# Moving activations and split weights 64 bytes apart in a 128-byte grid

## The chip, the core and the metric

The kernel runs on one NeuronCore of a Trainium2 chip. The metric is the device time of one execution in microseconds (us). A core has five engines that run side by side: TensorE (PE in the profile, with its weight loads listed as PEld), VectorE (DVE), ScalarE (ACT), GpSimd (POOL) and SyncE (SP, which here issues the DMAs). On-chip memory (SBUF) has 128 partitions. A tile takes the same range of byte addresses in every partition, so "the address of a tile" below is one number, its first byte within a partition.

## The reference, cut to what matters

Two layers of a transformer-like block over 256 tokens of width 1024, in float32. Each layer has a token mixer with three branches and an MLP:

```python
h = rms_norm(x, g_pre_mix) * (1.0 + sc_m) + sh_m
proj = h @ w_in                       # 1024 x 11272: rq rk rv rg lx ly fq fk fv ff gates
...                                   # retention, RG-LRU and forgetting attention
merged = g[:, :, 0] * (y_ret @ ret_w_o) + g[:, :, 1] * (y_lru @ lru_w_o) + g[:, :, 2] * (y_fox @ fox_w_o)
x = x + gt_m * rms_norm(merged @ w_out, g_post_mix)
h = rms_norm(x, g_pre_mlp) * (1.0 + sc_f) + sh_f
f = jnp.square(jax.nn.relu(h @ w1)) @ w2          # 1024 x 4096, 4096 x 1024
return x + gt_f * rms_norm(f, g_post_mlp)
```

Nearly all the work is matrix products of the 256 x 1024 activations with weights that are read once from memory. The shift, scale and gate columns come from further products with `ada_w`.

## The kernel before, in words

**Split operands.** Every float32 operand of a product is split into two float32r tiles, a high part and the remainder, and a product is three matmuls (`mm3`): high by high, high by low, low by high.

```python
def mm3(ps, ah, al, bh, bl, start, stop, **kw):
    T.matmul(ps, ah, bh, start=start, stop=False, **kw)      # L341
    T.matmul(ps, ah, bl, start=False, stop=False, **kw)      # L342
    T.matmul(ps, al, bh, start=False, stop=stop, **kw)       # L343
```

The first of the two operands is the stationary one: TensorE loads its 128 x 128 block with a weight load (LDWEIGHTS) ahead of each matmul. The second is the moving one, whose columns stream through.

**Two shapes of product.** `gemm` keeps a weight block stationary and streams 256 tokens of an activation (`hh`/`hl`, `yrh`/`yrl` and so on; the tiles in the profile's names stand in the order moving, stationary: `ps<-hh,whi`). `gemm_wide` and `gemm_n` keep 128 tokens of the activation stationary and stream the weights, 512 columns a matmul (256 in `gemm_n`; 264 in the one product of `fv` with the eight columns of `ff` beside it, whose output tiles are called `pf`). The MLP's `w2`, the first quarter of `w1`, `rv` and `w_o` take the wide form, the rest the other.

**Weights.** SyncE's queue brings each half of a weight block into one of five `wraw` tiles; `split` makes the high part on ACT (L217) and the remainder on DVE (L218). The pair goes to `whi`/`wlo` of the weight pool `wp`, or, where the table `SLOTS` or the list `SPARE_SLOTS` names a slot, into a `wown` tile in one of the activation slots.

**Activation slots.** The pool `up` has twelve slots of 8192 bytes per partition, `T1` to `T10`, `hh` and `hl`. `U(tag, shape, dt, name)` makes a tile in a slot. All activations that TensorE reads, except the small probability tiles `pth`/`ptl` and the gates' `uh`/`ul`, live there.

**Addresses.** The pools are laid out one after the other: `cpool` (constants, `sir`, the residual `xs`), `wp`, `up`, `tp` (scratch), `sp` (small columns). All tiles of `wp` and `up` begin at multiples of 128 bytes, and the rows within them are 512, 1024, 2048 or 4096 bytes long. One tile is an exception: `fv`'s first weight block is `[128, 4, 264]`, so its row `k` (one block of 128 input channels) begins 1056 `k` bytes, that is 32 `k` bytes past a multiple of 128. `sir` and `xs` begin 64 bytes past a multiple, since `csb` (8704 bytes) and `vsb` (1216 bytes) stand ahead of them. The constants' `csb` and `pth`/`ptl` begin at multiples.

**What sets the order.** The program is written out in one order (`mix_order`, `mlp_order`), weights are loaded two or three blocks ahead, and the work on heads is woven in between products by `side`. Each engine then runs its own list in order and waits on semaphores of the others.

Of the kernel before, what the change touches and what calls it, by code (L numbers as in the profile page):

```python
# [10 lines left out]
F32 = mybir.dt.float32  # L11
F32R = mybir.dt.float32r
# [2 lines left out]
ALU = mybir.AluOpType  # L15
PSUM = bass.MemoryType.PSUM
KH = 4
NRAW = 5
NHL = 4
PL = None  # L20
# [11 lines left out]
P = 128  # L32
D = 1024
KD = D // P
S = 256
L = 2
FF = 4 * D
NH_R = 4
NH_F = 8
C = 256  # L40
# [27 lines left out]
def mix_order(l):  # L68
    first = 'g0 g0 g0 g0 lx lx g1 lx g1 lx lru' if l == 0 else \
            'rv rv rv rv rq rk g0 rq rk g0 lx g0 lx g0 lx g1 lx lru g1'  # L70
    rest = 'rg rg rg rg g1 w_r w_r w_r w_r g1 ly ly ly ly fq w_l w_l w_l w_l fv fv fv fv fq fq fq fk fk fk fk ' \
           'g2 g2 g2 g2 w_f w_f w_f w_f w_o w_o w_o w_o'
    order = first.split() + rest.split()
    return [(n, order[:i].count(n)) for i, n in enumerate(order)]
# [8 lines left out]
def wide(name, cix):  # L83

    return name in ('rv', 'w_o', 'w2') or (name == 'w1' and cix < 4)
# [31 lines left out]
def trunk_kernel(ctx, tc, x, c, vec, con, ffw, wts, out):  # L117
# [4 lines left out]
    up = ctx.enter_context(tc.tile_pool(name="up", bufs=1))  # L122
# [5 lines left out]
    pz = ctx.enter_context(tc.tile_pool(name="pz", bufs=2, space=PSUM))  # L128

    V, A, T = nc.vector, nc.scalar, nc.tensor  # L130

    csb = cpool.tile([P, NCON], F32, name="csb")
    vsb = cpool.tile([P, L, NVEC], F32, name="vsb")
# [29 lines left out]
    both = cpool.tile([P, NH_F], F32, name="both")  # L163
# [35 lines left out]
    def raw_half(i, extra=None):  # L199
        n = C if extra is None else C + NH_F  # L200
        t = wp.tile([P, KH, n], F32, name="wraw", tag="wraw", bufs=NRAW)
        src = wts[pos[0], i]
        if extra is None:
            nc.sync.dma_start(t.rearrange("p k c -> p (k c)"), src)
        else:
            nc.sync.dma_start(t[:, :, :C], src.rearrange("p (k c) -> p k c", k=KH))
            nc.sync.dma_start(t[:, :, C:], extra[:, i * KH:(i + 1) * KH, :])
        return t
# [3 lines left out]
    def split_tiles(n):  # L212
        return (wp.tile([P, KH, n], F32R, name="whi", tag="whi", bufs=NHL),
                wp.tile([P, KH, n], F32R, name="wlo", tag="wlo", bufs=NHL))

    def split(t, hi, lo):
        A.copy(hi, t)  # L217
        V.tensor_tensor(lo, t, hi.bitcast(F32), ALU.subtract)  # L218
# [11 lines left out]
    def split_of(l, name, cix):  # L230
        parts = []
        for i in range(2):
            t = early.pop(0) if early else raw_half(i, ffw[l] if (name, cix) == ('fv', 0) else None)
            n = t.shape[-1]
            if (name, cix) in SLOTS:
                own = SLOTS[name, cix][i]
            elif name in ('w1', 'w2') and (name, cix) < ('w2', 12):
                own = SPARE_SLOTS[spare[0] % len(SPARE_SLOTS)]
                spare[0] += 1
            else:  # L240
                own = PL
            if own:
                both = U(own, [P, 2, KH, C], F32R, "wown")
                hi, lo = both[:, 0], both[:, 1]
            else:
                hi, lo = split_tiles(n)
            split(t, hi, lo)
            parts.append((hi, lo))
        pos[0] += 1
        if wide(name, cix):  # L250
            parts = [[p.rearrange("p (k j) c -> p k (j c)", k=2) for p in hl] for hl in parts]
            return [(parts[k // 2][0][:, k % 2, :], parts[k // 2][1][:, k % 2, :]) for k in range(KH)]
        return [(parts[k // KH][0][:, k % KH, :], parts[k // KH][1][:, k % KH, :]) for k in range(KD)]
# [143 lines left out]
            lates = [evac(banks[t][j], t, j) for j in range(2)]  # L397
        return lates

    def U(tag, shape, dt, name):  # L400
        return up.tile(shape, dt, name=name, tag=tag)

    def tmp(tag, name, dt=F32, shape=(P, 2, S), **kw):
        return tp.tile(list(shape), dt, name=name, tag=tag, **kw)
# [225 lines left out]
    def mixer(l, nm, h=None, rvp=None, qkp=None):  # L630
        hh, hl = h or nm.h

        def G(name, i, x=None, natural=False):
            prefetch(3 if name in DEEP else 2)
            side(BUDGET[name])
            w = weight(l, name, i)
            ps = pa.tile([P, 2, S], F32, name="ps", tag="a") if name in LONG else None
            return (gemm_n if natural else gemm)(w, *(x or (hh, hl)), ps)

        def pair(i):  # L640
            return slice(2 * i, 2 * i + 2)
# [55 lines left out]
        qk = {}  # L697
# [102 lines left out]

            first_quad(l, 'rv', nm, rv_quad)

        qk.update(rq=U("T1", [P, 2, NH_R, S], F32R, "rq"), rk=U("T2", [P, 2, NH_R, S], F32R, "rk"))
        heads = []

        def rope(name, i, ps):
            t = qk[name]
            sw = tmp("t1", "sw")
            A.copy(sw[0:64], ps[64:128])
            A.copy(sw[64:128], ps[0:64])  # L810
            r = tmp("t2", "ro")
            V.tensor_tensor(r, ps, cn('cos')[:, None, :].to_broadcast([P, 2, S]), ALU.mult)
            V.tensor_tensor(sw, sw, cn('sin')[:, None, :].to_broadcast([P, 2, S]), ALU.mult)
            yield 1.2
            V.tensor_tensor(r, r, sw, ALU.add)
            A.copy(t[:, 0, pair(i), :], r)
            lo(t[:, 1, pair(i), :], r, t[:, 0, pair(i), :])
            yield 1.2

        def add_heads(i, *after):  # L820
            heads.extend(Side(ret_head(h), *after, *heads[h - NPT:h - NPT + 1]) for h in (2 * i, 2 * i + 1))
            if i == 1:
                heads.append(Side(ret_norm(), *heads))
# [3 lines left out]
        def gate_evac(b, i):  # L827
            if i == 0:
                gate[b] = U("T9" if b else "T10", [P, KD, S], F32, "gate")
            A.activation(gate[b][:, pair(i), :], G(f'g{b}', i), AF.Tanh, scale=0.5)  # L830
# [133 lines left out]
        for n, i in mix_order(l):  # L964
            if n in ('rq', 'rk'):
                for _ in rope(n, i, G(n, i)):
                    pass
                if n == 'rk':
                    add_heads(i)
            elif n in ('g0', 'g1', 'g2'):  # L970
                gate_evac(int(n[1]), i)
            elif n == 'lx':
                if (l, i) == (0, 0):
                    lru_consts()
                conv(i)
            elif n == 'lru':
                for h in heads[:NH_R]:
                    finish(h)
                wl.append(weight(l, 'lru', 0))
                gs = [Side(lru_gates(j)) for j in range(4)]  # L980
            elif n == 'rg':
                if i == 0:
                    finish(heads[-1])
                    yr = U("T1", [P, KD, S], F32R, "yrh"), U("T2", [P, KD, S], F32R, "yrl")
                ret_gate(i, yr)
            elif n == 'w_r':
                if i == 0:
                    rec = Side(recurrence(), *gs)
                merge(0, 'w_r', i, yr)
            elif n == 'ly':  # L990
                if i == 0:
                    finish(rec)
                    yl = U("T3", [P, KD, S], F32R, "ylh"), U("T4", [P, KD, S], F32R, "yll")
                gelu_gate(i, yl)
            elif n == 'w_l':
                merge(1, 'w_l', i, yl)
            elif n == 'fq':
                if (l, i) == (0, 0):
                    V.tensor_tensor(both, ident[:, 0:NH_F], ident[:, CUM_LO:CUM_LO + NH_F], ALU.add)
                    A.mul(sel, both, -1.0)  # L1000
                if i == 0:
                    fq = U("T1", [P, NH_F, S], F32R, "fqh"), U("T2", [P, NH_F, S], F32R, "fql")
                fox_q(i, *fq)
            elif n == 'fv':
                if i == 0:
                    fv = U("T3", [P, 2, D], F32R, "fvh"), U("T4", [P, 2, D], F32R, "fvl")
                fox_v(i, *fv)
            elif n == 'fk':
                if i == 0:
                    fk = U("T5", [P, NH_F, S], F32R, "fkh"), U("T6", [P, NH_F, S], F32R, "fkl")  # L1010
                    yf = U("T7", [P, KD, S], F32R, "yfh"), U("T8", [P, KD, S], F32R, "yfl")
                fox_k(i, *fk)
            elif n == 'w_f':
                if i == 0:
                    side()
                    mh, ml = U("T1", [P, KD, S], F32R, "mh"), U("T2", [P, KD, S], F32R, "ml")
                    nm = Norms(l, 'm', (l, 'f'), ("T3", "T4", "T7"))
                merge(2, 'w_f', i, yf)
                ks = pair(i)
                A.mul(mh[:, ks, :], gate[0][:, ks, :], 0.5)  # L1020
                V.scalar_tensor_tensor(ml[:, ks, :], gate[0][:, ks, :], 0.5, mh[:, ks, :].bitcast(F32), ALU.mult,
                                       ALU.subtract)
# [163 lines left out]
```

## Time and profile before

| | |
|---|---|
| three runs | 1155.24, 1156.79, 2241.36 us; median 1156.79 |
| the profiled execution | 1157.0 us, its span 1155.2 us |
| TensorE busy | 1130.4 us, 98% of the span, 8164 matmuls |
| weight loads | 1066.6 us, 92% |
| DVE, ACT, POOL busy | 873.4 (76%), 617.9 (53%), 33.8 us (3%) |
| DMA | 255.43 MB, mean 221 GB/s |
| mean granted TensorE clock | 0.999 |

The span is what the profiler sees between the first and the last instruction; the execution's time holds 1.8 us more around it. Matmuls overlap in the profile: one is listed with the time from its issue to its end (some 283 ns for 256 columns), while the next one starts much earlier. How fast TensorE goes is therefore read from the distance between starts.

### The profile page before, as it was taken

The numbers are of one execution on the slowest core, as the hardware profiler recorded it, in microseconds if no ns is written. First come the engines' busy times: TensorE is split into PE (matmuls) and PEld (weight loads), VectorE is DVE, ScalarE is ACT, GpSimd is POOL, SyncE is SP. The second block draws the span as 40 slices with busy tenths as digits, with TensorE's granted clock in tenths as the row PEclk, the third lists the DMA queues.
The fourth block names the chain that finished last, engine by engine and source line by source line (L and its number), as shares of the span: only waits on it lengthen the run. The fifth ranks groups of instructions, "written<-read, shape, count | busy, mean of one in ns | idle before, by whom it ended". The sixth has DMA issues, their size and how long they took to land.

```text
span 1155.2 us, 20486 instructions
## 1 busy us (share of the span) xinstructions
PE 1130.4 (98%) x8164; PEld 1066.6 (92%) x8164; DVE 873.4 (76%) x1323; ACT 617.9 (53%) x912; POOL 33.8 (3%) x54
## 2 busy tenths in 40 slices
PE   6999999999999999999999999999999999999997
PEld 5999999999999889989879999999999997989986
DVE  6898788878787789887586768877777778866543
ACT  6676594544465555444555658655444645645432
POOL 0001000000000100000010010000000002000000
PEclk9999999999999999999999999999999999999999
DMA  9954546579876569998645454566777574875641
GB/s 364 390 181 148 183 135 210 180 245 315 282 242 221 194 221 320 335 308 297 236 157 172 151 194 148 167 199 185 232 264 253 180 276 146 274 244 187 192 150 67
DMA packets 74284, 255.43 MB, mean 221 GB/s; under 512 B 10108, under 2 KB 12492, under 8 KB 74188
## 3 DMA queue, kind: packets, MB, share of 16 engines
q1 hardware_dynamic: 74188, 254.12, 65.1%
q8 instruction: 64, 1.05, 0.4%
q14 instruction: 32, 0.26, 0.1%
HBM read 253.00 MB, written 1.09 MB: 220 GB/s over the span
## 4 chain that ended last, share of the span: by engine, by line
PE 82%; DMA 7%; DVE 4%; issue 4%; POOL 1%; ACT 1%; DVEq 0%; POOLq 0%; SPq 0%; ACTq 0%
PE ps L341 24%; PE ps L343 24%; PE ps L342 24%; DMA wraw<-in_wts_dram 7%; DVE wlo L218 2%; DVE wraw L273 1%; PE xT L421 1%; PE rvp L341 1%; PE rvp L342 1%; PE qkp L343 1%; PE qkp L341 1%; PE qkp L342 1%; PE rvp L343 1%; POOL rs_v L186 1%; POOL rs_r L187 0%
## 5 line engine op out<-in xcount | busy, mean ns | idle before, releaser
L217 ACT CAST whi<-wraw 128x1024 fp32r<-128x1024 f32 (+1 forms) x286 | 299.2, 1049 | 303.6 <-PE ps L342 184.7
L218 DVE TENSOR_TENSOR wlo<-wraw,whi 128x1024 fp32r<-128x1024 f32 (+1 forms) x286 | 348.3, 1222 | 109.9 <-ACT whi L217 108.5
L341 PE MATMUL ps<-hh,whi 128*128 128x256 f32 x1312 | 371.8, 283 | 2.2 <-DVE fvl L644 1.1
L343 PE MATMUL ps<-hh,wlo 128*128 128x256 f32 x1312 | 370.2, 282 | 0.0
L342 PE MATMUL ps<-hl,whi 128*128 128x256 f32 x1312 | 369.4, 282 | 0.0
L341 PEld LDWEIGHTS ps<-hh,whi 128*128 128x128 f32 x1312 | 249.3, 190 | 3.6 <-DVE fvl L644 1.5
L342 PEld LDWEIGHTS ps<-hl,whi 128*128 128x128 f32 x1312 | 249.1, 190 | 0.2
L343 PEld LDWEIGHTS ps<-hh,wlo 128*128 128x128 f32 x1312 | 249.2, 190 | 0.0
L273 DVE SCALAR_TENSOR_TENSOR wraw<-wraw,sir 128x1024 f32<-128x1024 f32 x82 | 100.0, 1222 | 38.6 <-DMA wraw<-in_wts_dram 38.2
L218 DVE TENSOR_TENSOR wown<-wraw,wown 128x1024 fp32r<-128x1024 f32 x72 | 87.1, 1222 | 26.1 <-ACT wown L217 25.4
L217 ACT CAST wown<-wraw 128x1024 fp32r<-128x1024 f32 x72 | 74.7, 1047 | 44.8 <-PE ps L343 30.9
L341 PE MATMUL ps<-whi,mih 128*128 128x512 f32 x144 | 56.6, 393 | 0.0
L343 PE MATMUL ps<-whi,mil 128*128 128x512 f32 x144 | 56.6, 393 | 0.0
L342 PE MATMUL ps<-wlo,mih 128*128 128x512 f32 x144 | 56.4, 392 | 0.0
L341 PE MATMUL ps<-whi,hh 128*128 128x256 f32 (+1 forms) x144 | 46.1, 320 | 0.0
L343 PE MATMUL ps<-whi,hl 128*128 128x256 f32 (+1 forms) x144 | 45.9, 319 | 0.0
L342 PE MATMUL ps<-wlo,hh 128*128 128x256 f32 (+1 forms) x144 | 45.9, 319 | 0.0
L343 PE MATMUL ps<-hh,wown 128*128 128x256 f32 x160 | 45.3, 283 | 0.0
L341 PE MATMUL ps<-hh,wown 128*128 128x256 f32 x160 | 45.3, 283 | 0.0
L342 PE MATMUL ps<-hl,wown 128*128 128x256 f32 x160 | 45.3, 283 | 0.0
L341 PE MATMUL ps<-wown,mih 128*128 128x512 f32 x112 | 43.7, 390 | 0.0
L342 PE MATMUL ps<-wown,mih 128*128 128x512 f32 x112 | 43.7, 390 | 0.0
(336 smaller groups left out, 2297.6 us busy)
## 6 DMA issues: line engine op xcount, KB each, us to landing
wraw<-in_wts_dram SPq DMA_DIRECT2D x440, 512.0 KB, 4.3
wfirst<-in_wts_dram SPq DMA_DIRECT2D x28, 512.0 KB, 9.8
rows<-drow SPq DMA_DIRECT2D x10, 512.0 KB, 5.1
xs<-in_x_dram SPq DMA_DIRECT2D x2, 512.0 KB
out_dram<-xs SPq DMA_DIRECT2D x4, 256.0 KB, 2.0
csb<-in_con_dram SPq DMA_DIRECT2D x1, 768.0 KB
csb<-in_con_dram SPq DMA_DIRECT2D x1, 256.0 KB, 9.3
vsb<-in_vec_dram SPq DMA_DIRECT2D x1, 152.0 KB
```

The lines of the kernel that those rows point to most:

```text
L186: eng.tensor_scalar(v, total, scale, EPS, ALU.mult, ALU.add)
L217: A.copy(hi, t)
L218: V.tensor_tensor(lo, t, hi.bitcast(F32), ALU.subtract)
L273: V.scalar_tensor_tensor(t, t, 0.5, sir, ALU.mult, ALU.mult, accum_out=m)
L341: T.matmul(ps, ah, bh, start=start, stop=False, **kw)
L342: T.matmul(ps, ah, bl, start=False, stop=False, **kw)
L343: T.matmul(ps, al, bh, start=False, stop=stop, **kw)
L421: i = T.transpose(pt[:, k, :], x[:, (k0 + k) * P:(k0 + k + 1) * P], ident)
```

## The change

A tile of 16 floats (64 bytes) is put ahead of the first slot of `up`, and each slot grows from 8192 to 8320 bytes, a multiple of 128. So all twelve slots now begin 64 bytes past a multiple of 128, and the pools behind `up` move by the same 64 bytes in the grid. A tile made with `other=True` starts 64 bytes further into its slot, at a multiple of 128 again. This is done for the split weights that live in activation slots (`wown`) and for `rk`, `fkh` and `fkl`, which meet other activations (`rq`, `fqh`, `fql`) in a matmul. `whi`/`wlo` stay at multiples of 128. The diff, whole but for its line numbers:

```diff
+PHASE = 16
...
     V, A, T = nc.vector, nc.scalar, nc.tensor
+    up.tile([P, PHASE], F32, name="phase")
...
             if own:
-                both = U(own, [P, 2, KH, C], F32R, "wown")
+                both = U(own, [P, 2, KH, C], F32R, "wown", True)
                 hi, lo = both[:, 0], both[:, 1]
...
-    def U(tag, shape, dt, name):
-        return up.tile(shape, dt, name=name, tag=tag)
+    def U(tag, shape, dt, name, other=False):
+
+        o, n = PHASE * other, math.prod(shape[1:])
+        t = up.tile([P, 2 * D + 2 * PHASE], dt, name=name, tag=tag)[:, o:o + n]
+        dims = {c: k for c, k in zip("abc", shape[1:])}
+        return t.rearrange(f"p ({' '.join(dims)}) -> p {' '.join(dims)}", **dims)
...
-        qk.update(rq=U("T1", [P, 2, NH_R, S], F32R, "rq"), rk=U("T2", [P, 2, NH_R, S], F32R, "rk"))
+        qk.update(rq=U("T1", [P, 2, NH_R, S], F32R, "rq"), rk=U("T2", [P, 2, NH_R, S], F32R, "rk", True))
...
-                    fk = U("T5", [P, NH_F, S], F32R, "fkh"), U("T6", [P, NH_F, S], F32R, "fkl")
+                    fk = U("T5", [P, NH_F, S], F32R, "fkh", True), U("T6", [P, NH_F, S], F32R, "fkl", True)
```

No instruction is added, removed or moved: the five engines' lists have the same instructions in the same order with the same waits before and after, and only addresses differ. Of 8144 matmuls in the program, 7997 had the start of their moving and stationary operands a multiple of 128 bytes apart before; 7993 have them an odd multiple of 64 bytes apart now. Most of the rest are matmuls whose stationary operand is one broadcast column, and the rows of `fv`'s first weight block: row 2 of each half of it (12 matmuls a layer, 24 in all) stood 64 bytes past the grid while the activation stood on it, and now both stand 64 bytes past.

## The prediction

> **What bounds the kernel now.** I read the busy row first, then the slices, then the chain that ended last.
>
> ```profile
> span 1155.2 us, 20486 instructions
> PE 1130.4 (98%) x8164; PEld 1066.6 (92%) x8164; DVE 873.4 (76%) x1323; ACT 617.9 (53%) x912; POOL 33.8 (3%) x54
> PE   6999999999999999999999999999999999999997
> DMA  9954546579876569998645454566777574875641
> PE 82%; DMA 7%; DVE 4%; issue 4%; POOL 1%; ACT 1%; DVEq 0%; POOLq 0%; SPq 0%; ACTq 0%
> PE ps L341 24%; PE ps L343 24%; PE ps L342 24%; DMA wraw<-in_wts_dram 7%; DVE wlo L218 2%; DVE wraw L273 1%; PE xT L421 1%; PE rvp L341 1%; PE rvp L342 1%; PE qkp L343 1%; PE qkp L341 1%; PE qkp L342 1%; PE rvp L343 1%; POOL rs_v L186 1%; POOL rs_r L187 0%
> ```
>
> TensorE is at nine tenths in every slice but the first and last, and holds 82% of the chain, nearly all of it in the three lines of `mm3`. So the kernel's time is the number of matmuls times the distance between their starts. No instruction is added or removed, hence the number stays, and the whole question is what the addresses do to that distance. Two per cent, about what a measurement of this kernel can tell from no change, is 23 us, or 23 / 8164 = 2.8 ns per matmul.
>
> The distance now, in one stretch of `w2` (512 columns a matmul) and two of `gemm` (256 columns), from the table of busy times by stretch (TensorE's busy time, matmuls that touch the stretch, granted clock, DMA share, GB/s):
>
> ```profile
> 449.05:471.07 22.02, 22.02 (x98) 1.00 0.95 328
> 516.04:538.98 22.94, 22.94 (x193) 1.00 0.87 308
> 694.01:814.05 120.04, 120.04 (x1010) 1.00 0.56 176
> ```
>
> A matmul is listed for 0.39 us where 512 columns stream and for 0.28 us where 256 do, so two or three that touch a stretch began before it. That leaves 96, 192 and 1007 starts: 229.4 ns for 512 columns, 119.5 and 119.2 ns for 256. How many there are of the wide kind, from the groups kept apart by shape (L341's, a third of all):
>
> ```profile
> L341 PE MATMUL ps<-whi,mih 128*128 128x512 f32 x144 | 56.6, 393 | 0.0
> L341 PE MATMUL ps<-wown,mih 128*128 128x512 f32 x112 | 43.7, 390 | 0.0
> L341 PE MATMUL ps<-whi,hh 128*128 128x512 f32 x48 | 19.0, 396 | 0.0
> L341 PE MATMUL ps<-wown,hh 128*128 128x512 f32 x48 | 19.0, 396 | 0.0
> L341 PE MATMUL ps<-wown,mh 128*128 128x512 f32 x32 | 12.7, 397 | 0.0
> L341 PE MATMUL ps<-whi,mh 128*128 128x512 f32 x32 | 12.5, 392 | 0.0
> L341 PE MATMUL rvp<-whi,hh 128*128 128x512 f32 x32 | 12.0, 429 | 2.1 <-ACT hh L484 2.1
> ```
>
> They are 448, so 1344 with L342 and L343. Of the other 6820 some 300 are transposes and other small ones; some 6500 stream 256 columns.
>
> **Is there anything to win?** The start of the run shows what streaming costs without haste (starts in us in the first column):
>
> ```profile
> 18.09 0.63 PE L343 MATMUL rvp<-whi,hl 128*128 128x512 f32 x1
> 18.52 0.63 PE L342 MATMUL rvp<-wlo,hh 128*128 128x512 f32 x1
> 18.95 0.44 PE L343 MATMUL rvp<-whi,hl 128*128 128x512 f32 x1
> ...
> 19.46 0.40 PE L343 MATMUL rvp<-whi,hl 128*128 128x512 f32 x1
> 19.69 0.40 PE L342 MATMUL rvp<-wlo,hh 128*128 128x512 f32 x1
> ```
>
> Matmuls of 512 columns start 0.43 us apart, and from 19 us on 0.23 us apart. If the early pace is half speed, streaming alone takes 215 ns at full speed, and 107.5 ns for 256 columns. The steady distances are 14.4 and 12 ns longer. The next matmul's weight load runs at the same time, so the excess may be two read streams in each other's way; it may also be the fixed cost of putting loaded weights to use, which no address changes. If all of it went: 1344 x 14.4 ns + 6500 x 12 ns = 19 + 78 = 97 us. That is the most the change can bring.
>
> The Trainium skill speaks against any of it: by its page "TensorE: Matmul & The Clock Gate", in the section "Step-by-step: what each phase is for", TensorE has two independent SBUF read ports, one for the streamed operand and one for weight loads, and loading the next weights takes nothing from the running matmul. By that rule the sum is 0. The same page gives 215.7 ns from start to start for 512 columns ("Wait — 56ns, not 53.3ns?"); here it is 229.4 ns with the clock at 1.00, so its picture misses 14 ns of this trace, and I do not rest the sum on it.
>
> **The place where the trace before already has the new distance.** `fv`'s first weight block has rows of 264 floats, 1056 bytes. Its row k starts 32k bytes past a multiple of 128, while the stationary `hh`/`hl` block starts at a multiple. Each row serves six matmuls (two token halves, three parts). So rows 2 and 6 of the eight run 64 bytes apart, just as nearly every matmul will after the change, and rows 0 and 4 run as nearly all do now. Row 4 begins the second half in a tile of its own. The first start of each row but the sixth, by the list in order of time:
>
> ```profile
> 245.82 0.29 PE L341 MATMUL pf<-whi,hh 128*128 128x264 f32 x1
> ...
> 246.55 0.28 PE L341 MATMUL pf<-whi,hh 128*128 128x264 f32 x1
> ...
> 247.27 0.29 PE L341 MATMUL pf<-whi,hh 128*128 128x264 f32 x1
> ...
> 247.99 0.28 PE L341 MATMUL pf<-whi,hh 128*128 128x264 f32 x1
> ...
> 248.71 0.29 PE L341 MATMUL pf<-whi,hh 128*128 128x264 f32 x1
> ...
> 249.45 0.28 PE L341 MATMUL pf<-whi,hh 128*128 128x264 f32 x1
> 250.18 0.29 PE L341 MATMUL pf<-whi,hh 128*128 128x264 f32 x1
> ...
> 250.91 0.29 PE L341 MATMUL pf<-whi,hh 128*128 128x264 f32 x1
> ```
>
> Row 0 takes 246.55 - 245.82 = 0.73 us, row 4 0.74 us. Row 2 takes 0.72 us and row 6 0.73 us. Odd rows, 32 or 96 bytes off, take 0.72 and 0.73 us. That is 121.7 and 123.3 ns a matmul on the grid, 120.0 and 121.7 ns at 64 bytes: 1.7 ns better, with a last digit that alone is worth 1.7 ns. Streaming 264 columns at the pace above takes 111 ns. If 64 bytes cleared the way, these rows would show some 0.67 us. They keep nine tenths of the excess.
>
> **The change part by part.**
>
> *Activations 64 bytes past, `whi`/`wlo` at a multiple.* This is the bulk. Unknown cost, bounded from both sides. Below: the 97 us. Above: no row shows a collision worse than now, and the nearest is the slowest row of `pf`, 123.3 ns; if 256 columns took as long as 264 do there, 6500 x 4 ns = 26 us are lost. Between ends this far apart I take the value of the row with the very distance, rows 2 and 6 of `pf`: no difference that its digits can tell, 0 us.
>
> *`wown` and `rk`, `fkh`, `fkl` moved back to a multiple.* They get the same answer, 0. Without this part they would just stay as they are, since both operands would have moved together.
>
> *DVE and ACT on tiles that start 64 bytes past.* DVE has done this all along: L273 reads `sir`, which starts 64 bytes past a multiple, beside `wraw` on the grid; L218's operands are all on it.
>
> ```profile
> L218 DVE TENSOR_TENSOR wlo<-wraw,whi 128x1024 fp32r<-128x1024 f32 x282 | 343.3, 1221 | 107.3 <-ACT whi L217 105.9
> L273 DVE SCALAR_TENSOR_TENSOR wraw<-wraw,sir 128x1024 f32<-128x1024 f32 x82 | 100.0, 1222 | 38.6 <-DMA wraw<-in_wts_dram 38.2
> ```
>
> 1221 and 1222 ns, so 0. ACT has no such pair of rows; at 53% busy it has room, and it would have to slow by far more than the excesses above before TensorE waited.
>
> *DMAs that land 64 bytes past.* The 28 `wfirst` transfers of the start do so now.
>
> ```profile
> wfirst<-in_wts_dram SPq DMA_DIRECT2D x28, 512.0 KB, 9.8
> ```
>
> They lie in the first 40 us, where the DMA row reads 9 and 9. Each partition's row is 4096 bytes; 64 more bytes touched in each would be 1.6% of 14.7 MB, or 0.24 MB. At the 328 GB/s of the first stretch above that is 0.7 us; nothing hides it there. Below nothing it cannot go, as no byte is saved. I take 0.
>
> The sum is 0 against the profiled execution's 1157.0 us (its span of 1155.2 and 1.8 around it). The median of the runs shown, 1156.8, agrees with it; I write 1156. The last digit of `pf`'s rows leaves 1.7 ns x 8164 = 14 us either way, so this case by itself reaches from 1142 to 1170.
>
> **The rivals.**
>
> *The offset clears the way.* If the two streams collide whenever they stand at the same place of a 128-byte period, half a period between them would keep them apart. For it: an excess of 12 to 14 ns that the slow start does not show. Against it: the `pf` rows, though they are only six matmuls each, with 264 columns, and a steady run may settle where a short one cannot. In full it is 97 us, but not all would arrive: the `w2` stretches already use 0.95 and 0.87 of the DMA engines, so they can shrink by 5 and 13% at most before weights come late. I count three quarters, 73 us: 1084 us.
>
> *It clears half the way*, because the pair differs in how long the streams overlap. Half of 97 us, 48 us, of which little is lost to DMA: 1110 us. For it speaks only that the rows of `pf` at 64 bytes are never the slowest.
>
> *Slower.* Two streams half a period apart may meet twice where they met once, and each weight load then ends later, and the next start with it. The place is `gemm`'s 6500 matmuls. Weight loads are listed so:
>
> ```profile
> L343 PEld LDWEIGHTS ps<-hh,wown 128*128 128x128 f32 x160 | 30.7, 192 | 0.0
> L342 PEld LDWEIGHTS ps<-wlo,mih 128*128 128x128 f32 x144 | 27.1, 188 | 5.9
> ```
>
> With 256 columns, a load of 192 ns starts every 119 ns and TensorE's load side is never idle; with 512 it is idle for part of the time, and the load takes 188 ns. So in `gemm` a load that is slowed further has no room. The rival decides from 2.8 ns on, where 119.3 becomes 122.1 ns; the slowest `pf` row, 123.3, is past that. At its 4 ns the loss is 26 us: 1183 us. Against it: rows 2 and 6 are not the slow ones.
>
> *The change doesn't do what it says.* The addresses do move for 7993 of 8144 matmuls, but the distance that counts could be another one: between a matmul's streamed operand and the next matmul's weights. In a product these two come from the same two kinds of tiles, so it is the same odd multiple of 64. This rival joins the forecast, at 1156.
>
> **How the numbers follow.** No difference that can be told: 0.52. All or most of the way cleared, 1084: 0.14. Half of it, 1110: 0.16. Slower, 1183: 0.18. So faster by over 2% is 0.30, within 2% is 0.52, slower 0.18. The range leaves out the 1084 case and takes in the half case and half or more of the slower one, up to 1182: from 1106 to 1182. The likeliest case alone has 1142 to 1170.
>
> **What would show it.** In the profile after, the same stretches of `w2` and `gemm` should again hold 96 and 192 starts in 22.0 and 22.9 us, and weight loads 188 to 192 ns. The offset clears the way if starts 256 columns apart fall towards 110 ns; then DVE or DMA should appear among what TensorE waits for in the `w2` stretches. The slower rival shows as 122 ns and more. L218 keeps its 1221 ns, or DVE does care where a tile starts. The prediction is wrong if a steady run of matmuls settles into another rhythm than six in a row do: that is the step on which it rests.

## The result, and the profile after

The change takes 1148.26 us, median of four runs (1147.38 to 1149.36), against 1156.14 us before. The ratio is 0.9935, with a 95% interval from 0.9915 to 0.9954: 0.65% faster, clear of noise and well inside 2%. The ratio leaves out one execution of before that took 2241.36 us. The head of the page after, with the chain by engine and by line:

```profile
span 1147.6 us, 20486 instructions
PE 1122.1 (98%) x8164; PEld 1055.2 (92%) x8164; DVE 872.4 (76%) x1323; ACT 616.6 (54%) x912; POOL 33.2 (3%) x54
PE 83%; DMA 6%; DVE 5%; issue 4%; ACT 1%; POOL 1%; DVEq 0%; POOLq 0%; SPq 0%; ACTq 0%
```

The span is 7.6 us shorter, TensorE's busy time 8.3 us, and nothing else has moved: the same number of matmuls stands closer together. The table by stretch (start and end in us, TensorE's busy time, matmuls that touch it, clock, DMA share, GB/s), before the change `w_f` of layer 0 and the second of two stretches of `w2`:

```profile
352.40:376.33 23.93, 23.93 (x203) 1.00 0.72 256
538.98:560.95 21.97, 21.97 (x98) 1.00 0.71 230
```

and then, of the change, `w_f`, the long stretch of `gemm` in layer 1, a `gemm` stretch of `w1`, and two stretches of `w2`:

```profile
350.46:373.32 22.86, 22.86 (x203) 1.00 0.79 255
690.33:808.89 118.56, 118.56 (x1010) 1.00 0.55 179
512.86:535.46 22.60, 22.60 (x193) 1.00 0.90 308
445.94:468.06 22.12, 22.12 (x98) 1.00 0.94 338
535.46:557.75 22.29, 22.29 (x98) 1.00 0.78 264
```

The stretches hold 201, 1007, 192, 96 and 96 starts, and the two of before 201 and 96. Three things stand in these rows. `gemm` starts are 117.7 ns apart (118.56 / 1007, 22.60 / 192) where they were 119.2 and 119.5. `w_f` alone went from 119.1 to 113.7 ns. The wide matmuls of 512 columns became slower: 230.4 and 232.2 ns where they were 229.4 and 228.9. Some 6500 x 1.6 ns = 10 us gained and 1344 x 1 to 3.3 ns = 1 to 4 us lost fit the measured 8.

`w_f` is the clue. With slots of 8320 bytes, 65 x 128, neighbouring slots differ by 128 bytes within a period of 256. So the high and the low part of an activation (`hh` and `hl`, `yrh` and `yrl`, `ylh` and `yll`) stand 128 apart in that period. The exception is `yfh`/`yfl`, in `T7` and `T8`, which were made in an order that puts both at 192.

The weights alternate too, and did so before the change: `whi` tiles are 4224 bytes apart, 33 x 128, so the two halves of a weight block stand at 0 and 128 in turn. Sorted by this, the long stretch before has its starts 120.0 ns apart where the operands are at the same place in 256 bytes and 118.3 ns where they are 128 apart; the first stretch of `w2` has 228.0 and 232.0 ns. The 119.2 and 229.4 ns are means of two rhythms, and places 128 bytes apart do not act alike.

DVE does not care where its tiles start. The row of the MLP's `mih`/`mil`, which the change moved by 64 and 192 bytes in the period, before and after:

```profile
L1041 DVE TENSOR_TENSOR mil<-mf,mih 128x512 fp32r<-128x512 f32 x24 | 16.4, 685 | 1.4 <-ACT mih L1040 1.4
L1047 DVE TENSOR_TENSOR mil<-mf,mih 128x512 fp32r<-128x512 f32 x24 | 16.5, 686 | 1.4 <-ACT mih L1046 1.4
```

### The profile page after: what moved, and what is told of

The parts are those of the page before. It is cut to its first block, busy times and chain, and to the rows that moved or that the text cites. A ratio compares the mean times of both kernels' runs of the same rounds, so it can differ in the third digit from the quotient of the medians.

```text
span 1147.6 us, 20486 instructions
## 1 busy us (share of the span) xinstructions
PE 1122.1 (98%) x8164; PEld 1055.2 (92%) x8164; DVE 872.4 (76%) x1323; ACT 616.6 (54%) x912; POOL 33.2 (3%) x54
## 4 chain that ended last, share of the span: by engine, by line
PE 83%; DMA 6%; DVE 5%; issue 4%; ACT 1%; POOL 1%; DVEq 0%; POOLq 0%; SPq 0%; ACTq 0%
PE ps L345 24%; PE ps L343 24%; PE ps L344 24%; DMA wraw<-in_wts_dram 5%; DVE wlo L220 2%; DVE wraw L275 1%; PE xT L427 1%; PE rvp L344 1%; PE rvp L345 1%; PE rvp L343 1%; PE qkp L344 1%; PE qkp L345 1%; PE qkp L343 1%; POOL rs_v L188 1%; ACT whi L219 0%
## 5 line engine op out<-in xcount | busy, mean ns | idle before, releaser
L343 PEld LDWEIGHTS ps<-hh,whi 128*128 128x128 f32 x1312 | 246.3, 188 | 4.3 <-PE ps L345 2.0
L220 DVE TENSOR_TENSOR wown<-wraw,wown 128x1024 fp32r<-128x1024 f32 x72 | 87.2, 1222 | 26.5 <-ACT wown L219 26.5
L343 PE MATMUL ps<-wown,mih 128*128 128x512 f32 x112 | 44.2, 395 | 0.0
L345 PE MATMUL ps<-wown,mil 128*128 128x512 f32 x112 | 44.1, 394 | 0.0
## 6 DMA issues: line engine op xcount, KB each, us to landing
wfirst<-in_wts_dram SPq DMA_DIRECT2D x28, 512.0 KB, 10.2
```

## The experiments

"Distance" is the distance between the stationary and the moving operand within a period of 256 bytes. The theories, as the expectations name them. **A**: what counts is this distance with a period of 256 bytes, and 64 bytes is best where it is the same for the high and the low part. **B**: only the 64 bytes to a 128-byte grid count, and `w_f` is fast for a reason of its own. **C**: the absolute start of the tiles counts. D and E came later. The ratios are to runs of the kernel before taken beside each experiment, whose medians were 1155.0 to 1155.6 us; the 1156.14 of the first row belongs to the change alone.

| run | us | ratio to before, 95% | 1007 starts of `gemm`, ns each | 96 starts of `w2`, ns each |
|---|---|---|---|---|
| before | 1156.14 | | 119.2 | 229.4 |
| the change | 1148.26 | 0.9935 (0.9915 to 0.9954) | 117.7 | 230.4 |
| slots of 8448 | 1133.95 | 0.9818 (0.9805 to 0.9832) | 113.5 | 229.9 |
| the change, weights in slots not moved | 1149.53 | 0.9958 (0.9945 to 0.9970) | 117.8 | 232.6 |
| all shifted by 64 | 1154.87 | 0.9994 (0.9984 to 1.0005) | 119.2 | 229.4 |
| slots of 8448, 32 bytes | 1150.01 | 0.9960 (0.9948 to 0.9973) | 117.1 | 233.4 |
| slots of 8320, no 64 bytes | 1153.74 | 0.9990 (0.9979 to 1.0001) | 118.4 | 231.7 |
| slots of 8448, 80 bytes | 1157.80 | 1.0030 (1.0017 to 1.0043) | 119.2 | 232.0 |
| wide at the activations' place, weights at one place | 1137.29 | 0.9848 (0.9833 to 0.9864) | 113.8 | 227.1 |
| the same, other sign | 1140.27 | 0.9874 (0.9855 to 0.9894) | 117.8 | 226.9 |
| slots of 8448, other sign | 1130.86 | 0.9788 (0.9774 to 0.9803) | 113.3 | 230.1 |
| wide at the activations' place, weights in turn | 1134.19 | 0.9816 (0.9798 to 0.9834) | 113.5 | 229.6 |
| slots of 8448, weights at one place | 1142.01 | 0.9877 (0.9857 to 0.9896) | 113.8 | 231.7 |

**Slots of 8448 bytes**, 33 x 256: the high and low parts of a pair stand at one place.

```diff
-        t = up.tile([P, 2 * D + 2 * PHASE], dt, name=name, tag=tag)[:, o:o + n]
+        t = up.tile([P, 2 * D + 4 * PHASE], dt, name=name, tag=tag)[:, o:o + n]
```

> The change with slots of 8448 bytes instead of 8320, so that every slot, the high and the low part's alike, begins 64 bytes past a multiple of 256. Theory A (a period of 256 bytes counts, and a matmul is fastest where the high and low parts stand at the same place in it, as only yfh/yfl of w_f do in the change's trace: 113.7 ns a start there, 117.7 elsewhere): all of gemm goes at some 113.7 ns, 6300 matmuls x 4 ns = 25 us less than the change, about 1123 us; the 512-column matmuls move by no more than 5 ns either way (7 us). Theory B (w_f is fast for another reason, the 64 bytes to the 128-byte grid are all that counts): 1148 us, as the change.

1133.95 us, 14 less than the change. `w_f`, the long stretch, `w2`, and an early `gemm` stretch of layer 0:

```profile
344.26:367.19 22.93, 22.93 (x202) 1.00 0.74 260
681.60:795.85 114.25, 114.25 (x1010) 1.00 0.58 185
439.60:461.67 22.07, 22.07 (x99) 1.00 0.94 332
95.02:115.69 20.67, 20.67 (x179) 1.00 0.56 178
```

The long stretch now goes at 113.5 ns, as `w_f` did in the change. Theory B falls. The gain is 11 us short of the 25 that A gave: the last row holds 178 starts at 116.1 ns, so part of `gemm` does not reach 113.5. A slower rhythm beside the fast one is what the later runs follow up.

**The change without moving the weights in slots.** `wown`, `rk`, `fkh` and `fkl` start where their slot starts.

```diff
-        o, n = PHASE * other, math.prod(shape[1:])
+        o, n = 0, math.prod(shape[1:])
```

> The change without its second half: wown, rk, fkh and fkl begin where the slot begins, 64 bytes past, so their matmuls (some 1300) have operands a multiple of 128 apart as before. Theory A and B: gemm on wown goes back from 117.7 towards 120 ns (480 matmuls, 1 us), the wide ones on wown back to the 229 of before from 231 or 232 (576 matmuls, 1 to 2 us less): within 3 us of the change, 1146 to 1150 us. If the second half carried the gain: 1155 us.

1149.53 us, as expected in total. The long stretch, whose weights are mostly `whi`/`wlo`, keeps its 117.8 ns. `w2` did not return to the 229 ns that was expected but went to 232.6, while the mean over all wide matmuls is 231.9 ns against the 231.6 of the change:

```profile
689.41:808.04 118.63, 118.63 (x1009) 1.00 0.55 178
444.78:467.11 22.33, 22.33 (x99) 1.00 0.92 324
```

The second half of the change is worth about 1 us, which these intervals cannot tell from nothing.

**All shifted by 64**, from the kernel before:

```diff
-    cpool.tile([P, 16], F32, name="pad")
```

> The kernel before without its unused 64-byte pad ahead of the weight pool: weights, activations and scratch all begin 64 bytes past a multiple of 128, so moving and stationary operands still stand a multiple of 128 apart. Theories A and B (the distance between the operands counts): 1156 us, as before. Theory C (the absolute start of the activations or of what DVE, ACT and DMA write counts): 1148 us, as the change, or another time than 1156.

1154.87 us, no difference, and the rhythm of before in both kinds of matmul:

```profile
693.26:813.28 120.02, 120.02 (x1009) 1.00 0.54 176
448.23:470.25 22.02, 22.02 (x98) 1.00 0.95 327
```

Theory C falls: where both operands move together, starting 64 bytes past the grid does nothing.

**32 and 80 bytes instead of 64**, with slots of 8448. The first edit:

```diff
-PHASE = 16
+PHASE = 8
...
-        o, n = PHASE * other, math.prod(shape[1:])
-        t = up.tile([P, 2 * D + 4 * PHASE], dt, name=name, tag=tag)[:, o:o + n]
+        o, n = (64 - PHASE) * other, math.prod(shape[1:])
+        t = up.tile([P, 2 * D + 64], dt, name=name, tag=tag)[:, o:o + n]
```

> As the run with slots of 8448 bytes, but activations begin 32 bytes past a multiple of 256 instead of 64 (the weights in slots still at a multiple of 256). Theory A with 64 bytes as the piece that counts: 32 bytes clear the way half, between 1123 and 1156, some 1140 us. If any offset off the grid does: 1123 us. Theory B: between 1148 and 1156 us.

1150.01 us; the long stretch at 117.1 ns, the wide matmuls at 233.4:

```profile
690.87:808.77 117.90, 117.90 (x1009) 1.00 0.55 180
445.32:467.73 22.41, 22.41 (x98) 1.00 0.95 341
```

The second edit:

```diff
-        o, n = PHASE * other, math.prod(shape[1:])
+        o, n = PHASE if other else 4, math.prod(shape[1:])
```

> The run with slots of 8448 bytes, with activations 80 instead of 64 bytes past a multiple of 256. Theory A with the exact half of 128 as the best place: slower than at 64, between 1134 and 1150 us (32 bytes gave 1150). If anything from 64 on clears the way: 1134 us.

1157.80 us, slower than expected and than before: 16 bytes beyond the best place and all of the gain is gone, 119.2 and 232.0 ns.

```profile
693.55:813.57 120.02, 120.02 (x1009) 1.00 0.55 176
447.65:469.92 22.27, 22.27 (x99) 1.00 0.95 329
```

So 64 bytes is not a threshold: of the offsets tried, 0, 32, 64 and 80, it is the best, and 80 has none of the gain. 48 and 96 were not run as offsets. Since the weights stand at 0 and 128 in turn, though, an offset of 32 is 96 to the other side for every second weight half, and one of 80 is 48.

**Slots of 8320 without the 64 bytes**, which keeps the alternating 128 and takes the rest of the change away.

```diff
-    up.tile([P, PHASE], F32, name="phase")
...
-        o, n = PHASE * other, math.prod(shape[1:])
+        o, n = 0, math.prod(shape[1:])
```

> The change without its 64 bytes: slots of 8320 bytes, all tiles at multiples of 128, so neighbouring slots stand 128 apart in a period of 256 and the high and low parts of a pair mostly differ by 128. Theory A (64 bytes is the gain, the alternating 128 is a loss): no faster than before; by the before trace's two rhythms (120 at 0, 118.6 at 128; 228 and 232 for the wide ones) between 1150 and 1162 us. If the slot size made the gain of the change: 1148 us.

1153.74 us, not to be told from before:

```profile
690.31:809.53 119.22, 119.22 (x1009) 1.00 0.56 177
445.33:467.57 22.24, 22.24 (x98) 1.00 0.95 338
```

The alternation alone gives `gemm` 0.8 ns (118.4 for 119.2) and costs the wide matmuls 2.3 ns. The change's loss on wide matmuls is at least in part this alternation, which comes with the slot size and not with the 64 bytes.

**Rows of 256 columns.** This run asks why `fv`'s rows misled the prediction: the same rows, 1056 bytes apart, but 256 columns a matmul.

```diff
-            gemm_n(weight(l, 'fv', 0), hh, hl, pf)
+            w0 = weight(l, 'fv', 0)
+            gemm_n([(a[:, :C], b[:, :C]) for a, b in w0], hh, hl, [p[:, :C] for p in pf])
+            gemm_n([(a[:, C:], b[:, C:]) for a, b in w0], hh, hl, [p[:, C:] for p in pf])
```

> The kernel before, where fv's first block streams its 256 columns in matmuls of their own, and the eight ff columns follow in 48 matmuls a layer of eight columns. The rows still start 32k bytes off the grid, six matmuls each, so rows 2 and 6 run 64 bytes apart for six matmuls of 256 columns. If the width of 264 columns hid the gain in the trace before: rows 2 and 6 at 113 to 115 ns a matmul after the first one or two, the others at 117 to 120. If six matmuls are too few to settle: rows 2 and 6 like the others, 118 to 121 ns. In total some 10 us more than before from the added small matmuls (96 at some 110 ns).

1169.96 us in its one run, 15 us over before (10 were expected for the added matmuls; behind those of layer 0 the granted clock is 0.71 from 257 to 268 us, which the estimate left out). What counts are the starts of row 2, row 3, row 6 and row 7:

```profile
248.08 0.28 PE L341 MATMUL pf<-whi,hh 128*128 128x256 f32 x1
...
248.79 0.28 PE L341 MATMUL pf<-whi,hh 128*128 128x256 f32 x1
...
250.92 0.28 PE L341 MATMUL pf<-whi,hh 128*128 128x256 f32 x1
251.04 0.28 PE L342 MATMUL pf<-wlo,hh 128*128 128x256 f32 x1
251.15 0.28 PE L343 MATMUL pf<-whi,hl 128*128 128x256 f32 x1
251.27 0.28 PE L341 MATMUL pf<-whi,hh 128*128 128x256 f32 x1
251.38 0.28 PE L342 MATMUL pf<-wlo,hh 128*128 128x256 f32 x1
251.49 0.28 PE L343 MATMUL pf<-whi,hl 128*128 128x256 f32 x1
251.61 0.28 PE L341 MATMUL pf<-whi,hh 128*128 128x256 f32 x1
```

Row 6 settles at once: five distances from 251.04 to 251.61, 114 ns each. Row 2, also 64 bytes apart, takes 0.71 us, 118 ns a matmul. Layer 1 repeats both. So six matmuls are enough to settle; it was the width of 264 that hid the gain in the trace before. And there are two rhythms at 64 bytes, some 113.5 and some 118 ns. The two rows differ in the sign of the distance: the weight tile of row 6 stands 128 bytes from that of row 2 in the period of 256.

The added matmuls of eight columns show something else. Each has its own weight load, and from the second to the thirtieth, at a clock of 1.00, they start 3.13 us / 28 = 111.8 ns apart, whatever the row:

```profile
252.34 0.25 PE L342 MATMUL pf<-wlo,hh 128*128 128x8 f32 x1
...
255.47 0.25 PE L343 MATMUL pf<-whi,hl 128*128 128x8 f32 x1
```

So a matmul with its load takes 112 ns here even where nearly nothing streams, and the 113.5 ns of the fast rhythm is within 2 ns of that.

**Wide blocks at the activations' place, all weights at one place.** By the rhythms so far, 512 columns want a distance of 0 and 256 columns one of 64.

```diff
-        return (wp.tile([P, KH, n], F32R, name="whi", tag="whi", bufs=NHL),
-                wp.tile([P, KH, n], F32R, name="wlo", tag="wlo", bufs=NHL))
+        o = PHASE * same
+        return [wp.tile([P, 2 * KH * C // 2 + 4 * PHASE], F32R, name=x, tag=x, bufs=NHL)[:, o:o + KH * n]
+                .rearrange("p (k c) -> p k c", k=KH) for x in ("whi", "wlo")]
...
-                both = U(own, [P, 2, KH, C], F32R, "wown", True)
+                both = U(own, [P, 2, KH, C], F32R, "wown", not wide(name, cix))
...
-                hi, lo = split_tiles(n)
+                hi, lo = split_tiles(n, wide(name, cix))
```

> The run with slots of 8448 bytes, but wide weight blocks (rv, w_o, w2, the first quarter of w1: 512 columns streamed) begin at the activations' place, 64 past a multiple of 256, so their matmuls have a distance of 0; and whi/wlo are 4352 bytes apart, a multiple of 256, so all weights of one kind stand at one place. Theory A with the rhythm being one of each distance and width (512 columns: 227 ns at a distance of 0, 230 at 64; 256 columns: 113.4 at 64): 1343 x 3 ns = 4 us less than the run with slots of 8448, about 1130 us. If the wide ones do not settle at 227: 1134 us.

1137.29 us. The wide matmuls did what A says, 227.1 ns; but a stretch of `gemm` in layer 0 went back to 117.8 ns (713 starts), while the long one in layer 1 kept 113.8:

```profile
443.37:465.17 21.80, 21.80 (x98) 1.00 0.94 341
158.90:242.88 83.98, 83.98 (x715) 1.00 0.57 183
685.21:799.81 114.60, 114.60 (x1009) 1.00 0.59 185
```

Two theories for the choice of rhythm. **D**: the sign of the distance decides. **E**: the way a stretch is entered decides, and a change of the weights' place from one weight half to the next gets it out of the slow rhythm.

**The other sign**, in that run and in the one with slots of 8448:

```diff
-    up.tile([P, PHASE], F32, name="phase")
+    up.tile([P, 3 * PHASE], F32, name="phase")
```

In the first of them the wide blocks move along (`o = 3 * PHASE * same`).

> The run with wide weights at the activations' place, with activations (and those weights) 192 instead of 64 bytes past a multiple of 256, all else the same. In gemm the stationary weights then stand 64 bytes past the streamed activations in the period of 256 (before this: 192 past). In the run with rows of 256 columns the row with that sign fell into the rhythm of 113 at once, the other one into 118. Theory D (two rhythms at half a period, and the sign of the distance decides which one a stretch falls into): gemm at 113.4 nearly everywhere, 6500 matmuls at 113.5 to 114 and the wide ones at 227: 10 to 20 us less than the 1137 of the other sign, about 1122 us. If the sign does not matter (the rhythm is set by how a stretch is entered): 1130 to 1140 us.

1140.27 us. The layer 0 stretch is now at 113.4 ns (722 starts), but the long one in layer 1 fell into 117.8:

```profile
157.71:239.62 81.91, 81.91 (x724) 1.00 0.59 189
685.06:803.66 118.60, 118.60 (x1009) 1.00 0.55 178
439.81:461.59 21.78, 21.78 (x98) 1.00 0.91 319
```

Theory D falls, as far as it says that the sign alone decides; the two stretches have just traded rhythms.

> The first run with slots of 8448 bytes, with activations 192 instead of 64 past a multiple of 256. The weights whi/wlo stand at 0 and 128 in turn as there, so both signs of the distance come equally often in either run, each on the other weight half. Under theory D and without it: about as that run, 1130 to 1138 us; the split weights in slots now have the favoured sign, which theory D counts at up to 2 us less.

1130.86 us, the best of all, at the edge of the expectation. Both stretches are in the fast rhythm:

```profile
159.27:240.09 80.82, 80.82 (x715) 1.00 0.61 189
681.80:795.93 114.13, 114.13 (x1010) 1.00 0.57 185
440.49:462.58 22.09, 22.09 (x99) 1.00 0.93 327
```

**Wide blocks and weights' place taken apart.** Both runs start from the one on wide blocks at 64 bytes. The first gives back the 4224 bytes between `whi` tiles, so that weights stand at 0 and 128 in turn; the second keeps 4352 bytes and gives back the wide blocks' distance.

```diff
-        return [wp.tile([P, 2 * KH * C // 2 + 4 * PHASE], F32R, name=x, tag=x, bufs=NHL)[:, o:o + KH * n]
+        return [wp.tile([P, KH * (C + NH_F)], F32R, name=x, tag=x, bufs=NHL)[:, o:o + KH * n]
```

> The first run with slots of 8448 bytes (activations 64 past a multiple of 256, whi/wlo 4224 bytes apart, so at 0 and 128 in turn), and wide weight blocks at the activations' place as in the run on them. Theory E (half a period apart there are two rhythms, 113.4 and 117.8; where the weights' place stays the same a stretch that has fallen into the slow one keeps it, and where it changes with each weight half it gets out): the starts 256 columns apart add up to some 760 us as in the first run, the wide ones to 315: about 1131 us. If it was the wide blocks' move that sent gemm into the slow rhythm: 256 columns at 769 us or more, 1137 us.

```diff
-                both = U(own, [P, 2, KH, C], F32R, "wown", not wide(name, cix))
+                both = U(own, [P, 2, KH, C], F32R, "wown", True)
...
-                hi, lo = split_tiles(n, wide(name, cix))
+                hi, lo = split_tiles(n)
```

> The first run with slots of 8448 bytes, but whi/wlo 4352 bytes apart, so that all weights stand at a multiple of 256 and no place alternates; the wide blocks stay half a period away. Theory E: gemm keeps the slow rhythm in several stretches, 256 columns at 769 us or more, about 1138 to 1142 us. If the wide blocks' move was the cause: 1134 us, as the first run.

1134.19 us with the weights in turn, 1142.01 us with them at one place. The first of them, layer 0 and layer 1:

```profile
158.30:239.12 80.82, 80.82 (x716) 1.00 0.57 190
682.35:796.60 114.25, 114.25 (x1010) 1.00 0.56 185
```

The second, layer 0 and a stretch of `w1` in layer 1, which went at 117.8 ns over all its 192 starts:

```profile
159.58:240.40 80.82, 80.82 (x715) 1.00 0.57 190
1021.92:1044.54 22.62, 22.62 (x193) 1.00 0.57 193
```

This is E's side in total time: with weights in turn the three runs take 1131 to 1134 us, at one place 1137 to 1142. Their distances of 256 columns add up to 743 to 747 us and 755 to 757. The wide blocks' move is not the cause.

The traces show the escapes themselves. These are the same 24 and 24 matmuls, two halves of one weight block in layer 0, first in the run with slots of 8448 (weights in turn), then in the first one with weights at one place:

```profile
101.98:104.80 2.82, 2.82 (x26) 1.00 0.53 177
104.80:107.52 2.72, 2.72 (x26) 1.00 0.32 127
103.33:106.15 2.82, 2.82 (x26) 1.00 0.55 190
106.15:108.98 2.83, 2.83 (x27) 1.00 0.28 113
```

With the weights' place the rhythm changes from 117.7 to 113.3 ns, at once; where the place stays, it stays too. Counted over all pairs of halves in `whi`/`wlo` without other work between them, in the three runs of each kind (a half is slow where the median of its last nine distances is 118 ns, fast where it is 113 or 114): at one place 5 of 294 slow halves are followed by a fast one. With weights in turn 67 of 101 are, where the change puts the weights 64 bytes past the activation, and none of 24 where it puts them 64 bytes before it. The way into the slow rhythm is the reverse: 18 of 196 fast halves with weights in turn are followed by a slow one where the weights then stand before the activation, 2 of 159 where they stand past it. So E holds, with a part of D: the change of place releases, but only towards one sign.

Moving the wide blocks also brought no gain where the weights are in turn (1134.19 against 1133.95): `whi` weights then stand 0 and 128 away in turn, and the wide matmuls go at 229.6 instead of 227.

## Why the prediction was right, and where it was wrong

The forecast was no difference beyond 2%, 1156 us, and it came out 8 us lower, inside both the range and the likeliest case's own 1142 to 1170.

*The bound* held: TensorE at nine tenths, the number of matmuls times their distance. It is the sum of all distances that counts, and not the one stretch of the table: the two runs with moved wide blocks and weights at one place differ by 4 ns in the long stretch, and yet their distances of 256 columns add up to 756.5 and 755.4 us, since other stretches went the other way round. (The 3 us between their times are not explained by these sums.)

*That the total came out within 2% is in part luck.* The same 64 bytes with slots 128 bytes longer gave a ratio of 0.9818, and with the other sign 0.9788 (0.9774 to 0.9803), on the edge of 2%. The prediction had no term for what the slot size does.

*"No difference that its digits can tell, 0 us"* is the step that failed. The sum took the rows of `pf` at 64 bytes for the bulk, and the bulk moved by 1.6 ns a matmul, 10 us, with 1 to 4 us lost on the wide ones. The rows were the right place to look and the wrong width: with 256 columns in the same rows one of the two that stand 64 bytes apart went at 114 ns. The doubt that the prediction named, that six in a row settle differently from a long run, was not the reason; they settle within one or two. Two slips in its working change no term: the DMA share of 0.87 belongs to the stretch of `gemm` in `w1` and not to `w2`, and the list of `pf` rows has the starts of all eight, and five matmuls lie between 249.45 and 250.18 us.

*"`wown` and the rest: 0"* held: 1.3 us between the two runs, which cannot be told from nothing.

*DVE on tiles 64 bytes past: 0* held, 685 and 686 ns where the tiles moved. The row that the prediction reads, L218, says little, since the change left its tiles where they were; in the run with everything shifted, which moved them, it has 1222 ns. ACT's `mih` has 620 and 621 ns. The `wfirst` DMAs went from 9.8 to 10.2 us in the change and in the run with everything shifted alike, and the latter's total does not differ from before.

*The rivals.* That the offset clears half the way was true of the mechanism, which this change only partly sets free: slots of 8320 bytes put the high and low parts 128 apart, and with slots of 8448 the time falls to 1134 us, with the other sign to 1131. The most that any version reached is 24 us of the 97. These 97 were too many: they let 256 columns go at 107.5 ns, and the matmuls of eight columns already take 111.8. By that row an estimate of the most is 6500 x 7.4 ns = 48 us for 256 columns in place of 78; the excess was in part what the prediction called the fixed cost of loaded weights. A slowing did appear, by 1 to 3 ns instead of 4, but in the 1344 wide matmuls and not in `gemm`, where the slower rival had put it; that weight loads end later is not shown.

*The rule of the Trainium skill* in "TensorE: Matmul & The Clock Gate", section "Step-by-step: what each phase is for", that a weight load takes no read bandwidth from the running matmul, does not agree with these runs as it stands: only the operands' places differ between them, and the distance of the starts moves between 113.3 and 119.2 ns. Moving both operands together changes nothing, so the two reads do act on each other. That what is lost is read bandwidth is not shown.

## What to carry to other kernels

Where a stream of float32r matmuls is the bound and its starts are some ns further apart than streaming takes, look at the addresses of the moving and the stationary operand within a period of 256 bytes. Of the places tried here, 256 columns want them 64 bytes apart, the same for all tiles that alternate as an operand (so slot sizes that are multiples of 256), and 512 columns want them at the same place. Let the place of the weights change from one half to the next, since a slow rhythm was left at such a change and hardly ever without one. And take a natural experiment in a trace only in the shape that the bulk has: a row of 264 columns said nothing about 256.

## What the runs showed of the hardware that was not expected

- The distance between starts settles into rhythms that depend on width and distance: 256 columns at 113.3 to 113.8 ns or 117.8 ns with 64 bytes between the operands, 120.0 with none and 118.3 with 128; 512 columns at 227 ns with none, 232 with 128 and some 229 to 233 with 64.
- Matmuls of eight columns, each with a weight load of 128x128, start 111.8 ns apart.
- At 64 bytes both rhythms exist for the same tiles: 1007 matmuls went at 113.8 ns in one run and at 117.8 in another in which only the sign of the distance differed, while 713 or so in the other layer did the opposite. A rhythm once entered lasts for hundreds of matmuls where the weights' place stays the same: 5 of 294 slow halves were left. Where the place changes, 67 of 101 were left towards weights 64 bytes past the activation, none of 24 towards weights 64 bytes before it. What lets the other 34 stay, and what in the memory makes the collision, stays open.
